# Transposing the retention operands one token block ahead, and splitting layer 1's output weights behind the GLA state chain

## The chip, the cores and the metric

The kernel runs on one core of a Trainium2 chip. The metric is the device time of one execution in microseconds (us), as the median of three runs. A core has a matrix engine (TensorE, PE in the profile), a vector engine (VectorE, DVE), a scalar engine (ScalarE, ACT), a general engine (GpSimd, POOL) and a sync engine (SyncE, SP) that issues most of the DMAs. PE writes to PSUM, the other engines take results from there.

## The reference

The kernel computes two layers of a diffusion backbone with model width 1024, for 512 latent tokens and 256 context tokens. Each layer projects the normalised tokens into three groups of heads (GLA, a gated linear attention; SSD, a state-space scan; retention), runs each as a scan in both directions, joins the outputs, projects them back and then runs a SwiGLU FFN. The two groups that matter here are instances of one scan, cut to its core:

```python
def chunked_scan(q, k, v, logg, s0):     # S_t = diag(exp(g_t)) S_{t-1} + k_t^T v_t,  o_t = q_t S_t
    def step(S, inp):
        qc, kc, vc, gc = inp
        G = jnp.cumsum(gc, axis=1)
...
        intra = jnp.einsum('bijh,bjhe->bihe', scores, vc)
        inter = jnp.einsum('bihd,bhde->bihe', qc * jnp.exp(G), S)
        G_last = G[:, -1:]
        S_new = jnp.exp(G_last[:, 0])[..., None] * S + jnp.einsum(
            'bjhd,bjhe->bhde', kc * jnp.exp(G_last - G), vc)
        return S_new, intra + inter
```

An output block is therefore a product inside the block (scores times values) plus a product of its queries with the state that enters it, once per direction. In the last layer only the four latent blocks are wanted as output; the two context blocks only feed the states.

## The kernel before

Tokens are handled in six blocks of 128: blocks 0 to 3 are latent, 4 and 5 context. Matrices of weights are loaded as fp32 into a buffer `raw`, of which there is one, and split into a high and a low part: ACT writes `whi`, DVE writes `wlo` as the rest. A product is then three matmuls (`gemm3`, L498): high by high, high by low, low by high.

The stage that is changed stands between the input projections and the FFN of each layer, and its code runs like this. `ret_gen` is a generator of the retention work, called by `pump()` from inside `gla_levels`, which builds the GLA scores level by level (L1016 to L1035: DVE, POOL and ACT make `XX`, PE multiplies it at L1028, DVE copies the masked result into `A` at L1035). For each output block `ret_out` does, on PE: four transposes of `qk` (L939); then, after DVE (L942) and ACT (L943, L944) have copied them to `rqT` in SBUF, the scores (L950), the products with the two states (L962), and, after DVE has multiplied the scores by their decay (`rA`, L953), the products with the values (L966); ACT copies the result to `vvg` (L968). `rqT` has one buffer.

After the retention come the GLA states. `gla_kv` (matmuls L1053, masked by DVE at L1057) makes what a block adds, `gla_step` (DVE, L1065) carries the state on, first backwards through the blocks, then forwards, and `gla_out` (L1073, L1077 on PE, L1083 on DVE) gives the outputs.

The output projection takes its weights in four units of 1024 by 256, loaded by `load_wo`: unit j is read into `raw` (L382) and split eight slices long (`whi` L394, `wlo` L395). `out_front` gates the joined block, transposes it (L1233), splits it into `H` (ACT L1235, DVE L1236) and multiplies it with the four units; the blocks are called positions 0 to 3 in layer 1. `out_back` normalises the rows (L283 and on), `load_gw` prepares a gain (POOL, L348).

The order on each engine isn't the order of the code: a scheduler simulates the program and takes, engine by engine, what it holds to be ready and due; the order within PE is filled up with matmuls of the remaining input projections (L498) where they fit. Engines work through their rows in that order. `tc.issue_after(x)`, used by the change, makes the instructions of the step's engine that are written inside it come behind instruction x in that order.

## Time and profile before

| what | us |
| --- | --- |
| median of three runs | 1889.72 |
| the three runs | 1876.48, 1889.72, 1896.44 |
| the profiled execution's own time | 1883.05 |
| its span, first to last instruction | 1881.3 |
| PE busy | 1744.7 |
| DVE busy | 1169.3 |
| ACT busy | 793.0 |
| POOL busy | 560.7 |

Times that are read from the profile belong to the profiled execution, which took 1883.05 us. The trace puts every instruction on its engine with a start and a length in microseconds from the start of the span, names what ended each wait, and gives the clock that TensorE was granted in any stretch as a share of its full speed (1.00 is 2.4 GHz, 0.50 is 1.2 GHz).

### The profile page before, as it was taken

How to read it: one execution, taken by the hardware profiler on the slowest of the kernel's cores; microseconds unless marked ns; L12 is line 12 of the kernel's file. 1: busy time of each engine (PE TensorE's matmuls, PEld its weight loads, DVE VectorE, ACT ScalarE, POOL GpSimd, SP SyncE). 2: the span in 40 equal slices, each digit the busy share in tenths (PEclk: the TensorE clock that was granted, in tenths of full speed). 3: DMA queues.
4: the chain of work that ended last, by engine and by line, in shares of the span. 5: the costliest groups of instructions: out<-in, count | busy, mean ns of one | idle time of the engine just before them, and what ended most of it. 6: DMA issues, size and time to landing. Idle time of an engine off the chain costs nothing. (4 is left out here: it accounts for less than half of the span.)

```text
span 1881.3 us, 30313 instructions
## 1 busy us (share of the span) xinstructions
PE 1744.7 (93%) x11851; PEld 1576.0 (84%) x11851; DVE 1169.3 (62%) x1981; ACT 793.0 (42%) x1433; POOL 560.7 (30%) x569
## 2 busy tenths in 40 slices
PE   4999999999879999999899989999987969999998
PEld 3778887798879999999788777889876969999886
DVE  4586787557557655554334446678766568888455
ACT  3545343225654333333323465444423544444343
POOL 1002622104303432332312240073312226555322
PEclk9999999999989999999999989999977989999999
DMA  8535457415325433332645374345613245444663
GB/s 277 183 103 171 136 188 262 156 46 177 113 68 145 140 105 93 93 93 90 240 140 184 116 235 134 112 147 171 214 53 124 84 129 153 125 138 130 245 209 128
DMA packets 239228, 275.15 MB, mean 146 GB/s; under 512 B 14056, under 2 KB 182476, under 8 KB 239084
## 3 DMA queue, kind: packets, MB, share of 16 engines
q1 hardware_dynamic: 237872, 271.30, 45.0%
q8 instruction: 93, 1.52, 0.3%
q10 hardware_dynamic: 1212, 1.91, 0.3%
q14 instruction: 51, 0.42, 0.1%
HBM read 234.24 MB, written 38.93 MB: 145 GB/s over the span
## 5 line engine op out<-in xcount | busy, mean ns | idle before, releaser
L369 DVE TENSOR_TENSOR wlo<-raw,whi 128x1024 fp32r<-128x1024 f32 (+2 forms) x192 | 264.1, 1382 | 160.0 <-ACT whi L368 159.7
L1324 PE MATMUL px<-H,whi 128*128 128x384 f32 (+1 forms) x1408 | 307.6, 310 | 7.4 <-ACT whi L368 7.3
L368 ACT CAST whi<-raw 128x1024 fp32r<-128x1024 f32 (+2 forms) x192 | 194.0, 1018 | 221.6 <-PE px L1324 86.3
L498 PE MATMUL mm<-whi,H 128*128 128x256 f32 x1376 | 275.5, 295 | 11.3 <-ACT stg L630 5.3
L498 PEld LDWEIGHTS mm<-whi,H 128*128 128x128 f32 x1376 | 224.1, 197 | 26.1 <-issue 12.7
L1324 PEld LDWEIGHTS px<-H,whi 128*128 128x128 f32 x1408 | 235.1, 190 | 10.2 <-ACT whi L368 9.5
L1324 PE MATMUL px<-H,wlo 128*128 128x384 f32 (+1 forms) x704 | 211.5, 310 | 0.9 <-DVE wlo L369 0.8
L498 PE MATMUL mm<-wlo,H 128*128 128x256 f32 x688 | 200.6, 292 | 0.0
L498 PE MATMUL mm<-H,whi 128*128 128x256 f32 (+2 forms) x640 | 160.9, 342 | 6.8 <-ACT xp L759 4.4
L368 ACT CAST whi<-S 128x1024 fp32r<-128x1024 f32 x88 | 73.5, 835 | 165.3 <-DVE S L419 84.6
L498 PEld LDWEIGHTS mm<-wlo,H 128*128 128x128 f32 x688 | 135.4, 197 | 3.1 <-issue 2.1
L1324 PEld LDWEIGHTS px<-H,wlo 128*128 128x128 f32 x704 | 131.6, 190 | 1.7 <-DVE wlo L369 1.7
L498 PEld LDWEIGHTS mm<-H,whi 128*128 128x128 f32 (+1 forms) x640 | 109.5, 190 | 26.0 <-ACT xp L759 6.2
L1278 POOL TENSOR_TENSOR hidlo<-hr,hidhi 128x768 fp32r<-128x768 f32 (+1 forms) x40 | 69.7, 1745 | 191.1 <-ACT hidhi L1277 184.7
L498 PE MATMUL px<-whi,H 128*128 128x256 f32 x640 | 120.5, 288 | 3.9 <-ACT H L1235 2.2
L1359 POOL TENSOR_TENSOR hf<-hf,g 128x384 f32<-128x384 f32 (+1 forms) x44 | 55.2, 1255 | 223.2 <-issue 147.0
L369 DVE TENSOR_TENSOR wlo<-S,whi 128x1024 fp32r<-128x1024 f32 x88 | 89.3, 1015 | 40.6 <-ACT whi L368 40.5
L1407 PE MATMUL px<-wlo,hidhi 128*128 128x512 f32 x276 | 108.7, 394 | 0.0
L498 PE MATMUL mm<-H,wlo 128*128 128x256 f32 (+3 forms) x320 | 108.3, 339 | 0.0
L1407 PE MATMUL px<-whi,hidhi 128*128 128x512 f32 x276 | 107.8, 393 | 0.0
L498 PEld LDWEIGHTS px<-whi,H 128*128 128x128 f32 x640 | 101.3, 193 | 6.3 <-ACT H L1235 3.2
L1407 PE MATMUL px<-whi,hidlo 128*128 128x512 f32 x276 | 106.1, 389 | 0.0
(334 smaller groups left out, 4086.0 us busy)
## 6 DMA issues: line engine op xcount, KB each, us to landing
raw<-ffn_w_dram SPq DMA_DIRECT2D x100, 512.0 KB
araw<-ada_w_dram SPq DMA_DIRECT2D x96, 512.0 KB
raw<-w_in_dram SPq DMA_DIRECT2D x26, 1024.0 KB
raw<-ffn_w_dram SPq DMA_DIRECT2D x20, 1024.0 KB
hr<-hd SPq DMA_DIRECT2D x22, 768.0 KB
hr<-hd SPq DMA_DIRECT2D x22, 512.0 KB
Rt<-gd SPq DMA_DIRECT2D x40, 256.0 KB
hd<-hf SPq DMA_DIRECT2D x22, 384.0 KB
```

The costliest lines, as they stand in the source:

```text
L368: S.copy(hi, src)
L369: lo_engine.tensor_tensor(lo, src, hi.bitcast(F32), ALU.subtract)
L498: PE.matmul(ps, x(k), y(k), start=(k == 0 and p == 0), stop=(k == total - 1 and p == 2))
L1278: (G if q else V).tensor_tensor(lo[:, q], hr[:, q], hi[:, q].bitcast(F32), ALU.subtract)
L1324: PE.matmul(ps[:, :hn], w[x][:, k], r[y](k), start=first and k == 0 and p == 0, stop=k == 3 and p == 2, skip_group_check=True)
L1359: G.tensor_tensor(h1, h1, g1, ALU.mult)
L1407: PE.matmul(ps, lh[x](k), rh[y](k), start=f + k == 0 and p == 0, stop=f + k == NF - 1 and p == 2, skip_group_check=True)
```

## The change

`ret_out` is cut in two. The new `ret_front` holds the transposes and the copies into `rqT`; it is called for the first output block ahead of the loop, and for every following block from inside the block before it, between the products with the states and the products with the values. In layer 1 `rqT` gets a second buffer. In layer 1, too, the splits of the output weights' units 1, 2 and 3 are held on DVE behind the fifth step of the GLA state chain (the last backward one; `steps` collects them, `chain` counts them). ACT's part of these splits is not held. No instruction is added or taken away.

```diff
-    def load(i, hp=None):
+    def load(i, hp=None, after=None):
...
-            for k in range(step):
-                w = cols[prem][:, 66 + k0 + k:67 + k0 + k]
-                S.activation(hi[:, k], raw[:, k0 + k], AF.Copy, scale=w)
-                V.scalar_tensor_tensor(lo[:, k], raw[:, k0 + k], w, hi.bitcast(F32)[:, k], ALU.mult, ALU.subtract)
+            with tc.issue_after(after) if after is not None else nullcontext():
+                for k in range(step):
+                    w = cols[prem][:, 66 + k0 + k:67 + k0 + k]
+                    S.activation(hi[:, k], raw[:, k0 + k], AF.Copy, scale=w)
+                    V.scalar_tensor_tensor(lo[:, k], raw[:, k0 + k], w, hi.bitcast(F32)[:, k], ALU.mult,
+                                           ALU.subtract)
...
-        def ret_out(tb, sf, sb):
-            qT = pt(Rp, "rqT", [128, 4, 2, 128], bufs=1)
+        def ret_front(tb):
+            qT = pt(Rp, "rqT", [128, 4, 2, 128], bufs=2 if last else 1)
...
             S.copy(qT[:, 0], pv[:, 0])
             S.copy(qT[:, 3], pv[:, 1])
+            return qT
+
+        def ret_out(tb, sf, sb):
+            qT = rq.pop(tb)
...
                     first = False
+            if tb != tbs_out[-1]:
+                nx = tbs_out[tbs_out.index(tb) + 1]
+                rq[nx] = ret_front(nx)
             for h in range(4):
                 PE.matmul(ps[:, 64 * h:64 * h + 64], A[:, h], vvg[:, tb, 256 + 64 * h:320 + 64 * h],
...
-                V.scalar_tensor_tensor(st, cur, g["dec"][d][:, i:i + 1], st, ALU.mult, ALU.add)
+                ins = V.scalar_tensor_tensor(st, cur, g["dec"][d][:, i:i + 1], st, ALU.mult, ALU.add)
+                steps.append(ins.ins)
...
             rf = None
+            rq[tbs_out[0]] = ret_front(tbs_out[0])
...
-            load(u["wo"][j], hp=None if j < 2 else wop)
+            load(u["wo"][j], None if j < 2 else wop, steps[chain - 1] if last and j else None)
...
                     gst_(t, t - 1 if t else None)
+                chain = len(steps)
```

The new text shifts line numbers: the retention's transposes, scores, state products and value products, L939, L950, L962 and L966 before, are L941, L956, L968 and L975 after; the level products L1028 become L1037, the projections' matmuls L498 become L500, the split L394 and L395 become L395 and L396, the GLA lines L1057, L1065 become L1066, L1074, and in the output projection L1208 to L1236 become L1220 to L1248.

On PE, in layer 1, this is the passage from the second to the third output block of the retention before the change (`rkv` are the states):

```order
L962 MATMUL px<-rkv_12817,rqT 128x128 x2
L962 MATMUL px<-rkv_12750,rqT 128x128 x2
L1028 MATMUL px<-XX 128x128 x4
L966 MATMUL px<-vvg,rA 128x64
L1028 MATMUL px<-XX 128x128 x2
L966 MATMUL px<-vvg,rA 128x64 x3
L1028 MATMUL px<-XX 128x128 x2
L939 MATMUL px<-cst,qk 128x128 x4
L950 MATMUL px<-rqT 128x128 x4
```

And the same passage, from the second output block to the third, after it:

```order
L968 MATMUL px<-rkv_12836,rqT 128x128 x2
L968 MATMUL px<-rkv_12773,rqT 128x128 x2
L500 MATMUL mm<-wlo,H 128x256
L941 MATMUL px<-cst,qk 128x128 x4
L1037 MATMUL px<-XX 128x128 x2
L500 MATMUL mm<-whi,H 128x256 x2
L975 MATMUL px<-vvg,rA 128x64
L1037 MATMUL px<-XX 128x128
L975 MATMUL px<-vvg,rA 128x64 x3
L1037 MATMUL px<-XX 128x128 x3
L500 MATMUL mm<-wlo,H 128x256
L500 MATMUL mm<-whi,H 128x256 x2
```

The transposes no longer stand directly ahead of the scores that need them, and matmuls of the last input projection (L500), which stood ahead of the first block before, stand between the blocks: 23 of them in the first of the three passages, 12 in the second, 5 in the third. In layer 0 the last three passages hold 44, 46 and 38 of these matmuls before and 14, 13 and 14 after, beside four transposes, four scores, four state products, four value products and eight level products in either; there, 141 of them now stand between the last GLA output and the first transposes of the output projection that follow.

On DVE, in layer 1, the GLA state chain before the change, from the third block's contribution on:

```order
L1057 TENSOR_TENSOR gkv_13202<-px,cst_10270 128x256
L395 SCALAR_TENSOR_TENSOR wlo<-raw,cols_645,whi 128x256
L1057 TENSOR_TENSOR gkv_13208<-px,cst_10270 128x512
L395 SCALAR_TENSOR_TENSOR wlo<-raw,cols_645,whi 128x256
L1065 SCALAR_TENSOR_TENSOR gkv_13202<-gkv_13196,gdec_12498,gkv_13202 128x256
L395 SCALAR_TENSOR_TENSOR wlo<-raw,cols_645,whi 128x256 x2
L1057 TENSOR_TENSOR gkv_13214<-px,cst_10270 128x512
L395 SCALAR_TENSOR_TENSOR wlo<-raw,cols_645,whi 128x256
L1057 TENSOR_TENSOR gkv_13219<-px,cst_10270 128x256
L395 SCALAR_TENSOR_TENSOR wlo<-raw,cols_645,whi 128x256
L1065 SCALAR_TENSOR_TENSOR gkv_13208<-gkv_13202,gdec_12498,gkv_13208 128x256
```

And after it, from the same block on to the first split:

```order
L1066 TENSOR_TENSOR gkv_13208<-px,cst_10270 128x512
L1074 SCALAR_TENSOR_TENSOR gkv_13202<-gkv_13196,gdec_12498,gkv_13202 128x256
L1066 TENSOR_TENSOR gkv_13214<-px,cst_10270 128x512
L1066 TENSOR_TENSOR gkv_13219<-px,cst_10270 128x256
L1074 SCALAR_TENSOR_TENSOR gkv_13208<-gkv_13202,gdec_12498,gkv_13208 128x256
L1074 SCALAR_TENSOR_TENSOR gkv_13219<-gkv_13191,gdec_12482,gkv_13219 128x256
L1074 SCALAR_TENSOR_TENSOR gkv_13214<-gkv_13208,gdec_12498,gkv_13214 128x256
L396 SCALAR_TENSOR_TENSOR wlo<-raw,cols_645,whi 128x256 x5
L1074 SCALAR_TENSOR_TENSOR gkv_13214<-gkv_13219,gdec_12482,gkv_13214 128x256
L396 SCALAR_TENSOR_TENSOR wlo<-raw,cols_645,whi 128x256 x3
```

The chain is no longer mixed with splits; the splits behind it are unit 1's, where those inside it before were unit 3's (and unit 2's ran just ahead of it).

On ACT, in layer 1, the rows between the last retention copy and position 0's `H`, after the change:

```order
L1220 ACTIVATE gt<-gt 128x512 x2
L1221 ACTIVATE zt<-zt 128x512
L1224 ACTIVATE zt,sy<-ys 128x512
L1225 ACTIVATE ys<-ys,rs 128x512
L1227 ACTIVATE zt<-vvg 128x512
L395 ACTIVATE whi<-raw,cols_645 128x256 x8
L1221 ACTIVATE zt<-zt 128x512
L1247 CAST H<-mm 128x512 x2
L1224 ACTIVATE zt,sy<-ys 128x512
L1227 ACTIVATE zt<-vvg 128x512
L1225 ACTIVATE ys<-ys,rs 128x512
L395 ACTIVATE whi<-raw,cols_645 128x256 x8
```

Unit 2's eight slices now stand ahead of position 0's `H` and unit 3's eight behind it; before, both units' slices stood ahead of it and ahead of L1215 (L1227 here). On SP the load of unit 2 into `raw` has moved behind the loads of `ys`, `gt` and `zt` of positions 0 and 1, and the load of unit 3 behind the loads of the rows `x`.

## Rows read from the trace of the kernel before

**Rows 1.** The page: busy time of the engines, and PE's clock in 40 slices.
```profile
PE 1744.7 (93%) x11851; PEld 1576.0 (84%) x11851; DVE 1169.3 (62%) x1981; ACT 793.0 (42%) x1433; POOL 560.7 (30%) x569
...
PEclk9999999999989999999999989999977989999999
```

**Rows 2.** Layer 1: window, length, busy PE, PEld, DVE, ACT, POOL, clock, DMA.
```profile
1370.00:1380.00 10.00, 10.00 (x85) 9.42 (x82) 6.90 (x22) 4.55 (x13) 0.00 (x0) 1.00 0.09 30
1380.00:1390.00 10.00, 7.99 (x55) 6.76 (x54) 6.99 (x20) 2.92 (x7) 1.74 (x4) 0.52 0.37 118
...
1430.00:1440.00 10.00, 3.69 (x13) 3.37 (x14) 7.24 (x17) 2.95 (x8) 0.00 (x0) 0.58 0.19 54
```

**Rows 3.** Waits from 1366 to 1460 us: engine, line, releaser, total, times, longest.
```profile
PE px L1073 <- DVE gkv L1065: 8.0, 1, 8.0
...
PE px L950 <- ACT rqT L944: 5.6, 3, 2.0
```

**Rows 4.** PE's timeline in layer 1: start, length, line, operands, idle before.
```profile
1382.86 1.11 PE L939 MATMUL px<-cst,qk 128*128 128x128 f32 x4
1385.99 1.22 PE L950 MATMUL px<-rqT 64*128 64x128 f32 x8 [2.01 <-ACT rqT L944]
...
1394.68 1.11 PE L939 MATMUL px<-cst,qk 128*128 128x128 f32 x4
...
1400.63 0.84 PE L1028 MATMUL px<-XX 32*128 32x128 f32 x8
...
1403.86 0.69 PE L939 MATMUL px<-cst,qk 128*128 128x128 f32 x4
```

**Rows 5.** PE's timeline after the retention, to the output projection's first two positions.
```profile
1414.02 2.07 PE L1028 MATMUL px<-XX 32*128 32x128 f32 x20
...
1436.31 2.05 PE L1073 MATMUL px<-gkv,qe 128*128 128x256 f32 x4 [7.99 <-DVE gkv L1065]
...
1449.72 0.39 PE L498 MATMUL px<-whi,H 128*128 128x256 f32 x1 [1.20 <-ACT H L1235]
...
1462.96 0.38 PE L498 MATMUL px<-whi,H 128*128 128x256 f32 x1 [0.38 <-ACT H L1235]
```

**Rows 6.** DVE's timeline in the GLA state chain of layer 1.
```profile
1427.31 0.42 DVE L1057 TENSOR_TENSOR gkv<-px,cst 128x256 f32<-128x256 f32 x1
1430.19 0.48 DVE L395 SCALAR_TENSOR_TENSOR wlo<-raw,cols,whi 128x256 fp32r<-128x256 f32 x1 [2.46 <-ACT whi L394]
1430.59 0.68 DVE L1057 TENSOR_TENSOR gkv<-px,cst 128x512 f32<-128x512 f32 x1
...
1435.68 1.78 DVE L1065 SCALAR_TENSOR_TENSOR gkv<-gkv,gdec,gkv 128x256 f32<-128x256 f32 x4
```

**Rows 7.** Unit 3's load on SP's queue, and its split on ACT.
```profile
1424.03 0.38 SPq L382 DMA_DIRECT2D raw<-w_out_dram  x1
...
1429.65 3.30 ACT L394 ACTIVATE whi<-raw,cols 128x256 fp32r<-128x256 f32 x8 [2.38 <-DMA raw<-w_out_dram]
```

**Rows 8.** Layer 0's output weights: load, ACT's split, DVE's split, POOL's gain beside it.
```profile
445.76 0.38 SPq L382 DMA_DIRECT2D raw<-w_out_dram  x1
...
453.06 3.31 ACT L394 ACTIVATE whi<-raw,cols 128x256 fp32r<-128x256 f32 x8 [4.56 <-DMA raw<-w_out_dram]
...
454.60 7.06 DVE L395 SCALAR_TENSOR_TENSOR wlo<-raw,cols,whi 128x256 fp32r<-128x256 f32 x7
...
456.37 5.01 POOL L348 TENSOR_TENSOR gw<-gw,xn 128x1024 f32<-128x1024 f32 x2 [4.90 <-DMA gw<-gts]
```

**Rows 9.** Windows of L498 alone: window, length, PE busy, PEld busy, clock.
```profile
1350.00:1355.00 5.00, 1.35 (x9) 1.15 (x10) 1.00 0.59 169
1355.00:1360.00 5.00, 1.58 (x12) 1.17 (x10) 1.00 0.56 199
1375.00:1380.00 5.00, 1.00 (x7) 0.65 (x5) 1.00 0.04 11
```

**Rows 10.** One window of layer 0's retention and GLA, all engines.
```profile
350.00:440.00 90.00, 90.00 (x737) 81.64 (x736) 50.51 (x128) 26.95 (x60) 15.00 (x26) 1.00 0.19 63
```

More of the change, by code (lines that the diff above doesn't have):

```diff
@@ L1 @@
-from contextlib import ExitStack
+from contextlib import ExitStack, nullcontext
 import numpy as np
@@ L1083, in gla_out @@
             V.tensor_tensor(vvg[:, tb, 0:256], y, ps[:, :256], ALU.add)
-        gA = {}
-        rkv, rb = {}, {5: None}
+        gA, steps = {}, []
+        rkv, rb, rq = {}, {5: None}, {}
         def ret_gen():
```

## The prediction

> **What bounds the kernel now.** The page comes first. PE is busy for 1744.7 of 1881.3 us, 93%, and no other engine above 62%, so nearly everywhere PE's own work sets the time and a change off PE is worth nothing [rows 1]. In the row of PE's clock the reader is to see the one deep dip, the slices that read 7 and 7 late in the line: one slice is 47 us, so they lie between 1364 and 1458 us. That is layer 1's retention and GLA, the stage of this change. Next come the windows there: until 1380 PE is fully busy at a clock of 1.00, then it is busy for 8 of 10 us at 0.52, and in 1430 to 1440 for 3.69 of 10 [rows 2]. So two losses overlap, waits and half speed. The waits name their releasers: three of them, 5.6 us together, are scores that wait for ACT's last copy into `rqT`, and one of 8.0 us is the first GLA output waiting for the state chain on DVE [rows 3]. Layer 0 does the same work in 350 to 440 us with PE busy for 90.00 of 90 us at 1.00 [rows 10]: there the change removes no wait of PE.
>
> **The change part by part.** I make the sum against the profiled execution, 1883.05 us (span 1881.3, the rest lies around it), and move its difference to the median, 1889.72, which is 6.7 us above it; the three runs themselves span 20 us, so nothing under 1% (19 us) can be told from no change.
>
> *The transposes, layer 1.* Each passage between blocks now reads transposes (L939), PE idle, scores (L950) [rows 4]. With the transposes ahead of the value products, these and the level products stand as cover over DVE's and ACT's copies: in the first passage of before, 7.5 us of products lie between the end of the scores (1387.21) and the next transposes (1394.68), and of these only the state products stay ahead of the transposes; the copies' wait is 2.01. The three waits go: -5.6 us [rows 3]. Their work is moved, not removed. What comes late next is `rA`, DVE's product between scores and value products; the state products, and now the transposes too, cover it. The second `rqT` buffer lets the copies start without waiting for the state products. If the cover were gone, the 5.6 would come back.
>
> *The clock, layer 1.* Without waits, the three passages from 1382.86 to 1414.02 hold 31.16 - 5.6 = 25.6 us of work, of which 1400.63 to 1404.55 ran at full speed [rows 4, 5]; so 21.6 us ran at half, and could shrink by 10.8. Whether they do hangs on what PE does there, and the matmuls of the projection, L498, now stand among them (23, 12 and 5). One costs 1.35/9 = 0.15 us at full clock [rows 9]. The rows show two stretches of mixed work to compare with: in 1350 to 1360, with 21 records of L498 among level products, the clock was 1.00 and stayed there; in 1375 to 1380 there were 7, and behind it the clock fell [rows 2, 9]. A passage has half of 9.8 us (11.82 less its 2.01 of waiting) = 4.9 us of other work at full clock. The first, 23 matmuls in 8.4 us, is nearest to the stretch that kept its clock, the third, 5 in 5.7 us, to the one behind which it fell, and the second, 12 in 6.7 us, lies between. Both ends: nothing regained, and 40 matmuls at half speed besides (+6.0), or 10.8 regained. I take the first passage alone at full speed, -4.9, and the 17 matmuls of the others at half speed, 17 x 0.15 = +2.6.
>
> *The state chain, layer 1.* DVE's rows show 7.95 us from the end of one L1057 (1427.73) to the last steps (1435.68); in them DVE idles 2.46 for `whi`, whose slices wait for unit 3's load, and eight splits stand between the chain's own instructions at 0.40 each (1430.19 to 1430.59) [rows 6, 7]. All of this leaves the chain: -(2.46 + 3.2) = -5.7. PE waits 7.99 for just this [rows 5], so the whole of it is on the path. Unit 2's eight splits stood ahead of the chain, beside the last level copies; they are worth between 0 and 3.2, as these copies were partly waiting for PE anyway, and I take the middle, -1.6.
>
> *What is given back.* DVE's splits of units 1 to 3 now start at the fifth step, before 1436.6 (1435.68 plus half of the last four steps' 1.78) [rows 6]. There is one `raw`, so each unit's load, on SP's queue, waits for the splits of the unit before it. From the fifth step: 3.2 for unit 1's splits and 0.4 for a step between them, 5.6 for unit 2's load (1424.03 to 1429.65), 3.3 for ACT's slices, which are queued ahead of position 0's `H` [rows 7], and 1.2 from `H` to the first matmul [rows 5]: 13.7 us, where it was 1449.72 - 1436.6 = 13.1. Thus the GLA outputs, which set this stretch before, are overtaken by the weights: +0.6. Unit 3 follows: its load can start at some 12.9, its first slice is split at 12.9 + 5.6 + 0.8 = 19.3, and position 0, which takes about 12 us (the 13.24 between the first matmuls of two positions, less the 1.2), needs it after three quarters, at 13.7 + 9 = 22.7 [rows 5]. So 3.4 us remain, and the loads of the FFN's weights behind it on SP have longer still. Layer 0's load took 7.3 (445.76 to 453.06) [rows 8], so one load may be late by 1.7 and shift all of it. And seven splits took 7.06 us there, not 2.8, while POOL wrote two gains in 5.01: 4.3 longer, 2.1 for the one gain of layer 1. Ends: 0 and 3.8; I take 1.7, the slower load. Together +2.3.
>
> The Trainium skill, "SBUF — State Buffer", section "SBUF: two separate sides", has it that VectorE and GpSimd share a pair of ports which whoever comes first holds for a whole instruction. Layer 0's seven splits agree with it [rows 8]; by that rule the late splits meet POOL's gain surely, and the sum would lose the 2.1 as well, 10.8 in the place of 12.9.
>
> *Layer 0.* Its waits aren't in the retention, but the order moves: the fill goes from the passages (44 to 14 in each of the last three) to the stretch ahead of the output projection, 141 x 0.15 = 21 us. At full clock this is neutral. The output weights' splits then lie beside other work; what can be won or lost is bounded by those seven splits' 4.3 us, either way. I take 0.
>
> **The sum:** -5.6 - 4.9 + 2.6 - 5.7 - 1.6 + 2.3 = -12.9 us: 1870.2 for the profiled execution, 1876.8 on the median.
>
> **The rivals.** *The clock stays up through all of layer 1's passages:* -5.6 - 10.8 - 7.3 + 2.3 = -21.4, 1868.3. For it speaks that PE will have no waits there; against it, that the fall at 1380 came behind 10 us in which PE was busy without a gap [rows 2], and that the third passage is made of nearly the same matmuls as before. The Trainium skill, "TensorE: Matmul & The Clock Gate", section "HAM oscillation — how this bites in real kernels", lays such falls to stretches in which TensorE idles, so that taking the waits away would give this rival. This trace shows a fall without one.
>
> *The clock doesn't come back and the weights come late:* -5.6 + 6.0 - 7.3 + 2.3 = -4.6 with the weights as I took them, and -2.5 with the other end of what is given back (0.6 + 3.8); some -3, 1886.7. For it speaks that the scores, level and value products are the same matmuls that ran at 0.5 before.
>
> *Slower, through layer 0:* the last three passages there, 14 matmuls of L498 (2.1 us) beside 4.9 us of other work, fall to half speed as layer 1's did. Each then takes 14 us and not 7: +21.0, and with the -12.9 of layer 1 +8.1, 1897.8. It decides at the point where such a passage loses its full clock. Against it, 14 in 7.0 us is near the 21 in 10 us of the stretch that stayed at 1.00; for it, that stretch had other products beside the level products, and what never fell in layer 0 before had about 44 in 11.5 us [rows 9, 10].
>
> That the change doesn't do what it says is excluded: the order shows the moved rows on PE, DVE, ACT and SP.
>
> **How the numbers follow.** Forecast 0.45, full clock 0.20, clock and weights 0.20, layer 0 slower 0.15. The predicted time is the forecast's, 1876.8. The range reaches down to 1864, a little under the full-clock case with layer 0's 4.3 on its side, and up to 1895, over the weights' case and most of the way to the slower one. Faster by over 1% means under 1870.8: two thirds of the full-clock case (0.13) and a fifth of the forecast (0.09), 0.22. Slower by over 1%, above 1908.6, takes layer 0 falling for longer than three passages: 0.07. Within 1%: 0.71.
>
> **What would show it.** After: no wait of L956 for `rqT`; no split between L1066 and L1074, and the wait of the GLA outputs (8.0) down to 2 or so; clock 1.00 for the first passage, about 0.5 in the third; the first output matmul 13 to 14 us behind the fifth step, waiting for ACT's `H`, and this in turn for the load; clock 1.00 in layer 0's retention. Wrong would be: a wait of that size on `rA` or on PSUM, a clock under 0.9 between 350 and 440 us, or a period of positions 0 to 1 well above 15 us.

## The result and the profile after

The changed kernel takes 1905.18 us (median of four runs, 1893.48 to 1915.39) and the one before 1890.01 (four runs, 1876.48 to 1896.44): a ratio of 1.0105, interval 1.0068 to 1.0142. It is slower by one per cent, where 1876.8 had been forecast, and it lies above the range. The profiled execution took 1896.16 us with a span of 1894.4, 13.1 more than before. The four executions had spans of 1894.4, 1912.4, 1891.7 and 1913.6 us at mean granted clocks of 0.955, 0.946, 0.956 and 0.947: of the 20 us between the two pairs some 18 are half speed, and the profiled execution is one of the shorter pair.

The page of the kernel after, busy time of the engines and PE's clock in 40 slices:

```profile
PE 1765.8 (93%) x11851; PEld 1592.7 (84%) x11851; DVE 1165.9 (62%) x1981; ACT 792.7 (42%) x1433; POOL 562.9 (30%) x569
...
PEclk9999999999898999999999989999978979999999
```

The number of instructions is the same as in [rows 1], and PE is busy for 21.1 us longer with them. The row of the clock doesn't tell where: the slices over layer 0's retention (350 to 440 us) read 9 in both kernels, since one slice is 47 us and averages a fall of 10 us away. The new 8 in the 11th slice lies at 474 to 521 us, behind the retention, and the 8 of the 12th has moved to the 13th. The dip in layer 1 is still there.

One window over layer 0's stage, from 330 us, where the two kernels still stand at the same place, to its last transposes of L306, before and then after (columns as in [rows 2]):

```profile
330.00:552.20 222.20, 203.75 (x1656) 186.40 (x1652) 124.79 (x285) 92.23 (x197) 49.19 (x66) 0.97 0.35 118
```

```profile
330.00:568.80 238.80, 220.94 (x1644) 200.61 (x1636) 123.64 (x285) 92.07 (x197) 50.01 (x66) 0.92 0.33 108
```

The stage grew by 16.6 us. PE's idle time in it didn't (18.4 before, 17.9 after, length less busy time): no wait was won or lost. What changed is the clock. The time lost by it is taken as the length times what the clock lacks of 1.00, PE's waits counted in; summed over windows of 5 us it is 7.4 us before and 19.0 after. So 11.6 of the 16.6 us are half speed. Narrower windows of the kernel after show where:

```profile
350.00:360.00 10.00, 10.00 (x77) 8.58 (x76) 5.49 (x18) 1.93 (x5) 0.76 (x2) 1.00 0.05 16
...
370.00:380.00 10.00, 10.00 (x54) 8.98 (x54) 7.94 (x17) 2.56 (x5) 2.21 (x5) 0.52 0.08 22
...
420.00:430.00 10.00, 10.00 (x53) 9.10 (x53) 3.33 (x8) 1.94 (x3) 1.45 (x2) 0.75 0.15 39
...
460.00:470.00 10.00, 7.08 (x33) 6.59 (x34) 6.88 (x16) 7.51 (x17) 3.68 (x4) 0.66 0.56 170
...
500.00:510.00 10.00, 8.16 (x50) 8.16 (x51) 7.60 (x16) 9.10 (x18) 6.19 (x6) 0.66 0.64 209
```

Of these the reader is to see the second: PE is busy for 10.00 of 10 us and runs at 0.52. Nothing in PE's busy column tells it from the window in the first row; the count of matmul records does (54, not 77). And the same 90 us as in [rows 10]:

```profile
350.00:440.00 90.00, 90.00 (x602) 79.17 (x600) 51.66 (x127) 20.76 (x45) 14.39 (x26) 0.91 0.12 38
```

PE is busy for 90.00 us as before, with 602 matmul records in place of 737.

In layer 1 the same stage, from the L306 transposes ahead of it to those at its end, before and after:

```profile
1110.00:1514.50 404.50, 371.06 (x2744) 329.50 (x2743) 269.65 (x547) 181.45 (x372) 104.49 (x140) 0.92 0.42 133
```

```profile
1126.70:1525.70 399.00, 373.11 (x2743) 331.27 (x2742) 267.55 (x546) 180.99 (x371) 104.70 (x140) 0.93 0.42 134
```

It gained 5.5 us: PE's idle time fell by 7.5 (33.4 to 25.9) and its busy time rose by 2.1. With layer 0's +16.6 this is +11.1 of the +13.1; the rest, 1.9, stands behind layer 1's stage (1894.4 - 1525.7 against 1881.3 - 1514.5). What became of layer 1's waits, from 1390 to 1490 us of the kernel after:

```profile
PE px L500 <- ACT H L1247: 3.9, 1, 3.9
PE mm L1245 <- DVE gt L1234: 2.4, 1, 2.4
...
PE px L1083 <- DVE gkv L1074: 1.7, 1, 1.7
```

The three waits for `rqT` (5.6 in [rows 3]) are gone, and the wait for the state chain has gone from 8.0 to 1.7. In their place stand a wait for `gt` ahead of position 0's transposes and one for position 1's `H`. PE's timeline shows the two new ones and the first output matmul:

```profile
1440.33 1.10 PE L1083 MATMUL px<-gkv,qe 128*128 128x256 f32 x4 [1.69 <-DVE gkv L1074]
...
1452.79 0.69 PE L1245 MATMUL mm<-cst,gt 128*128 128x128 f32 x2 [2.37 <-DVE gt L1234]
...
1454.58 0.58 PE L500 MATMUL px<-whi,H 128*128 128x256 f32 x1
...
1471.98 0.39 PE L500 MATMUL px<-whi,H 128*128 128x256 f32 x1 [3.89 <-ACT H L1247]
```

From the first output matmul of position 0 to that of position 1 it is 17.4 us, where [rows 5] have 13.24. ACT's and DVE's rows say what stands ahead of the `gt` and the `H`; ACT first:

```profile
1449.49 3.30 ACT L395 ACTIVATE whi<-raw,cols 128x256 fp32r<-128x256 f32 x8 [3.54 <-DMA raw<-w_out_dram]
...
1462.77 3.31 ACT L395 ACTIVATE whi<-raw,cols 128x256 fp32r<-128x256 f32 x8 [2.63 <-DMA raw<-w_out_dram]
...
1468.59 0.63 ACT L1224 ACTIVATE zt<-ys 128x512 f32<-128x512 f32 x1 [0.90 <-DVE ys L1222]
...
1471.36 1.06 ACT L1247 CAST H<-mm 128x512 fp32r<-128x512 f32 x2
```

And DVE's:

```profile
1450.87 1.27 DVE L396 SCALAR_TENSOR_TENSOR wlo<-raw,cols,whi 128x256 fp32r<-128x256 f32 x3
1452.05 0.68 DVE L1234 TENSOR_TENSOR gt<-gt,hss 128x512 f32<-128x512 f32 x1
...
1463.31 3.28 DVE L396 SCALAR_TENSOR_TENSOR wlo<-raw,cols,whi 128x256 fp32r<-128x256 f32 x8 [1.59 <-ACT whi L395]
1467.15 1.41 DVE L1222 TENSOR_TENSOR ys<-ys,zt 128x512 f32<-128x512 f32 x1 [0.56 <-ACT zt L1221]
```

Three splits of unit 2 stand directly ahead of position 0's `gt`. The eight of unit 3 stand ahead of position 2's `ys` (position 1's `gt` was done at 1461.7, ahead of them). Position 1's `H` is late on ACT: it stands there behind unit 3's slices, which wait for their load, and behind position 2's gating, which waits for that `ys`.

### The profile page after: what moved, and what is told of

It reads as the page before. It is cut to its first block, busy times and chain, and to the rows that moved or that the text cites. A ratio compares the mean times of both kernels' runs of the same rounds, so it can differ in the third digit from the quotient of the medians.

```text
span 1894.4 us, 30305 instructions
## 1 busy us (share of the span) xinstructions
PE 1765.8 (93%) x11851; PEld 1592.7 (84%) x11851; DVE 1165.9 (62%) x1981; ACT 792.7 (42%) x1433; POOL 562.9 (30%) x569
## 4 chain that ended last, share of the span: by engine, by line
PE 64%; DMA 14%; DVE 10%; ACT 5%; issue 3%; POOL 3%; SPq 0%; POOLq 0%; ACTq 0%; DVEq 0%
PE px L1336 17%; PE mm L500 16%; PE px L1419 6%; PE mm L1336 6%; PE px L500 5%; DMA raw<-ffn_w_dram 5%; DVE wlo L369 3%; PE px L1037 2%; DMA qd<-stg 2%; DMA araw<-ada_w_dram 2%; PE mm L1419 2%; ACT whi L368 2%; DMA raw<-w_out_dram 1%; DMA raw<-w_in_dram 1%; PE pa L203 1%
## 5 line engine op out<-in xcount | busy, mean ns | idle before, releaser
L500 PE MATMUL mm<-whi,H 128*128 128x256 f32 x1376 | 283.7, 299 | 12.7 <-ACT stg L632 6.7
L500 PEld LDWEIGHTS mm<-whi,H 128*128 128x128 f32 x1376 | 227.8, 199 | 31.2 <-issue 13.7
L500 PE MATMUL mm<-wlo,H 128*128 128x256 f32 x688 | 203.5, 296 | 0.0
L500 PE MATMUL mm<-H,whi 128*128 128x256 f32 (+2 forms) x640 | 161.2, 342 | 6.6 <-ACT xp L761 5.5
L500 PEld LDWEIGHTS mm<-wlo,H 128*128 128x128 f32 x688 | 137.2, 199 | 3.3 <-issue 2.5
L500 PE MATMUL px<-whi,H 128*128 128x256 f32 x640 | 125.1, 295 | 8.3 <-ACT H L1247 4.5
L500 PEld LDWEIGHTS mm<-H,whi 128*128 128x128 f32 (+1 forms) x640 | 109.4, 190 | 26.4 <-ACT xp L761 7.4
L500 PEld LDWEIGHTS px<-whi,H 128*128 128x128 f32 x640 | 104.9, 200 | 11.4 <-ACT H L1247 5.7
L500 PE MATMUL mm<-H,wlo 128*128 128x256 f32 (+3 forms) x320 | 108.5, 339 | 0.0
```

The costliest lines, as they stand in the source:

```text
L500: PE.matmul(ps, x(k), y(k), start=(k == 0 and p == 0), stop=(k == total - 1 and p == 2))
```

## The experiments

The diffs are against the changed kernel unless the text names another, and show the lines that matter. Ratios are to the kernel before, from runs on the same chip, with the 95% interval. The theory after the result was: layer 0's retention runs at half speed because the order moved the projections' matmuls out of it; layer 1's gains are real and partly given back. The rivals were that layer 0's part costs nothing and layer 1's weights come so late that they cost the per cent, and that the falls of the clock wander from execution to execution and the change has no part in them.

**Fronts ahead in layer 0 alone.** Layer 1 keeps the order of before, in both parts.

```diff
...
-            qT = rq.pop(tb)
+            qT = ret_front(tb) if last else rq.pop(tb)
...
-            if tb != tbs_out[-1]:
+            if not last and tb != tbs_out[-1]:
...
-            load(u["wo"][j], None if j < 2 else wop, steps[chain - 1] if last and j else None)
+            load(u["wo"][j], None if j < 2 else wop, None)
```

> Only layer 0's transposes go ahead; layer 1 is as before, both in order and in weights. Theory A (the loss is layer 0's new order: matmuls of the projection leave the retention, the scores and level products are cut into more and shorter groups, and the clock falls in this stage): slower than before by 14 to 22 us, 1.0075 to 1.0115, with the clock at half speed somewhere between 360 and 430 us and the first out-projection transposes some 17 us later than 443.6. Rival B (the falls of the clock wander from execution to execution and the change has no part in it): within 5 us of before.

It gave 1.0127 (1.0100 to 1.0154): all of the loss, from a part that was to cost nothing. Its window over layer 0's stage:

```profile
330.00:581.50 251.50, 232.94 (x1666) 210.28 (x1664) 123.61 (x285) 92.44 (x198) 50.05 (x66) 0.89 0.32 104
```

and the 90 us of [rows 10] in it:

```profile
350.00:440.00 90.00, 90.00 (x547) 77.69 (x547) 41.67 (x107) 17.18 (x36) 9.56 (x20) 0.79 0.11 36
```

Half speed costs 28.0 us here (again over windows of 5 us), 20.6 more than before. This is the longest of six executions; what half speed takes in all of them stands in the table at the end of this section.

**Layer 1 alone, both parts.** Layer 0 keeps the order of before.

```diff
-            qT = rq.pop(tb)
+            qT = rq.pop(tb) if last else ret_front(tb)
...
-            if tb != tbs_out[-1]:
+            if last and tb != tbs_out[-1]:
```

> Both parts of the change, in layer 1 alone; layer 0 as before. Theory A: layer 1's gain in the profile stands by itself, 5 us (the waits of 5.6 and 6.3 us less 5.3 us of new waits in the output projection and some slower matmuls), so 0.995 to 1.000, and layer 0's clock at 1.00 from 350 to 440 us. Rival B: as far off as the changed kernel, 1.005 to 1.015.

1.0009 (0.9986 to 1.0031): no gain that can be measured, and just above the 0.995 to 1.000 expected. With the 1.0127 of layer 0 the two halves make 1.0136, within the interval of the whole change. PE's waits in its layer 1:

```profile
PE mm L1246 <- DVE gt L1235: 3.8, 1, 3.8
PE px L500 <- ACT H L1248: 3.6, 3, 3.0
...
PE px L500 <- DVE H L1249: 2.1, 3, 0.7
```

These are the new waits for `gt` and `H` again, 9.5 us together.

**The transposes ahead in layer 1 alone,** the weights split as before.

```diff
-            qT = rq.pop(tb)
+            qT = rq.pop(tb) if last else ret_front(tb)
...
-            if tb != tbs_out[-1]:
+            if last and tb != tbs_out[-1]:
...
-            load(u["wo"][j], None if j < 2 else wop, steps[chain - 1] if last and j else None)
+            load(u["wo"][j], None if j < 2 else wop, None)
```

> Only layer 1's transposes go ahead; the weights are split as before. If the transposes' cover is what I took it for, the three waits for rqT (5.6 us) go and the state chain's 8.0 us stay; the scores are cut apart by projection matmuls, which gives 1 to 2 us back: 0.996 to 0.999. If the cut scores and the clock eat it all: 0.999 to 1.002.

0.9965 (0.9947 to 0.9982), -6.6 us. This part gains by itself.

**The weights alone.** No front ahead in either layer.

```diff
-            qT = rq.pop(tb)
+            qT = ret_front(tb)
...
-            if tb != tbs_out[-1]:
+            if False and tb != tbs_out[-1]:
...
-            rq[tbs_out[0]] = ret_front(tbs_out[0])
```

> Only layer 1's weight splits go behind the state chain; the transposes stay. The chain's wait falls from 8.0 to about 1.7 us. If the output projection's new waits (5.3 us in the changed kernel: 2.9 in front of its matmuls, 2.4 in front of its transposes) come from the late weights, they are here too, and the time is within 2 us of before: 0.999 to 1.001. If they come from the transposes' part, the gain of 6 us stands: 0.995 to 0.998.

0.9976 (0.9957 to 0.9994), -4.5 us. The gain stands, and yet the wait for `gt` is here too (2.4 us), so that it comes with the weights and not with the transposes. Each part of layer 1 gains, and both together don't. The summary of the output projection's matmuls (first and last start) shows where the gain goes; the kernel before, with the transposes alone, with the weights alone, and with both:

```profile
L498 PE MATMUL px<-whi,H x256: 278/283/388, 1449.7 to 1501.0; 128*128 128x256 f32 x128
```

```profile
L500 PE MATMUL px<-whi,H x256: 278/283/387, 1435.2 to 1486.5; 128*128 128x256 f32 x128
```

```profile
L500 PE MATMUL px<-whi,H x256: 274/283/582, 1450.4 to 1504.7; 128*128 128x256 f32 x128
```

```profile
L500 PE MATMUL px<-whi,H x256: 277/283/581, 1434.2 to 1496.7; 128*128 128x256 f32 x128
```

The projection takes 51.3, 51.3, 54.3 and 62.5 us. Its start is counted from the last of the L306 transposes ahead of the stage (1109.7, 1103.0, 1113.6 and 1108.8), since the spans differ up to there: 340.0 us before, 7.8 earlier with the transposes alone, 3.2 with the weights alone, 14.6 with both. So the gains ahead of the output projection do add up, and more; but with both, 11.2 of the 14.6 are given back in it. One window over the projection, before and with both, says by what:

```profile
1449.70:1501.00 51.30, 50.90 (x423) 50.28 (x424) 27.94 (x49) 27.72 (x55) 14.72 (x15) 1.00 0.36 123
```

```profile
1434.20:1496.70 62.50, 56.38 (x425) 54.32 (x424) 30.51 (x60) 31.94 (x65) 14.71 (x15) 0.92 0.33 111
```

PE's idle time grew by 5.7 us (0.4 to 6.1), the waits for `H` above, and 5.0 are half speed; for the weights themselves PE waits nowhere. In the changed kernel the start is 11.7 earlier (1454.6 less 1126.3), the projection takes 57.6, and 6.3 are given back: 4.0 of idle time and 2.3 of half speed. The profiled execution with both parts is one of the shorter of its twelve (a span of 1876.9, 4.4 under before's), so that it still shows some gain where the median shows none.

**Only unit 3 held back.** Units 1 and 2 are split as before; the transposes ahead in layer 1 alone.

```diff
-            load(u["wo"][j], None if j < 2 else wop, steps[chain - 1] if last and j else None)
+            load(u["wo"][j], None if j < 2 else wop, steps[chain - 1] if last and j == 3 else None)
```

> Layer 1's transposes ahead, as in the changed kernel; layer 0 as before; and of the weight splits only unit 3's are held behind the state chain, so that units 1 and 2 are split early and their loads no longer wait for the chain. If layer 1's gain was lost in the chain of load, split and load again (unit 2's load after unit 1's splits, unit 3's after unit 2's), the chain's wait stays at about 2 us, the 8.8 us of waits in front of the output projection's transposes and matmuls fall to 2 or 3 us, and the time is 9 to 13 us under before: 0.993 to 0.996. Rival: the two parts don't add because the clock falls elsewhere in their place; then it is no better than the transposes alone, 0.996 to 0.999.

And the same on the kernel before, with nothing else:

```diff
-            load(u["wo"][j], hp=None if j < 2 else wop)
+            load(u["wo"][j], None if j < 2 else wop, steps[chain - 1] if last and j == 3 else None)
```

> Only unit 3's splits are held behind the state chain; transposes as before, in both layers. By the same theory the chain's 8.0 us fall to about 2 and nothing is given back: 4 to 7 us under before, 0.9965 to 0.998. If holding units 1 and 2 as well costs nothing, the same as the kernel that holds all three (0.9976).

They gave 0.9960 (0.9939 to 0.9980), at the edge between its theory and its rival, and 0.9987 (0.9966 to 1.0007), which misses the 0.9965 to 0.998 expected. The second is no better than all three units held (0.9976), so that by itself it decides nothing. With the transposes ahead, one unit held beats three (0.9960 against 1.0009, the intervals apart), and it is not to be told from none held (0.9965). So with the transposes ahead holding the weights is worth nothing, and holding all three costs.

**The projections' matmuls brought forward.** On the kernel with fronts ahead in layer 0 alone, the projections that fill layer 0's retention are given a higher priority, so that they run ahead of it and none is left to stand in the passages.

```diff
-        proj_b("gr", tbs_out, to_dram(rds[l], 0))
-        proj_b("rg", tbs_out, to_dram(rds[l], 256))
-        for j in range(2):
-            proj_b(f"z{j}", tbs_out, to_dram(zds[l], 256 * j))
+        with tc.high_priority(offset=1000) if not last else nullcontext():
+            proj_b("gr", tbs_out, to_dram(rds[l], 0))
+            proj_b("rg", tbs_out, to_dram(rds[l], 256))
+            for j in range(2):
+                proj_b(f"z{j}", tbs_out, to_dram(zds[l], 256 * j))
```

> Layer 0's transposes ahead, layer 1 as before; and the projection matmuls of layer 0 that follow the retention in the code are raised in priority, so that they all run ahead of the retention: its last three passages hold none of them, and the scores are no longer cut apart. Theory clock (what the stage lost is full speed, since the fill is gone from the passages): no better than the kernel with 14 of them in each passage, 1.010 to 1.020, with 0.5 in most of the last three passages. Theory cut (what it lost is the cutting of scores and level products into short groups): 8 us better than that kernel, 1.005 to 1.009, and the scores back at half their time.

1.0213 (1.0185 to 1.0241), the worst of all and a little above either theory's range. In the last three passages, with scores at 450, 458, 466 and 473 us here, no matmul of the projections is left; in the first two, from 422, some still stand. Windows ahead of the passages, in the first two, and from the last three on:

```profile
360.00:370.00 10.00, 10.00 (x48) 5.87 (x49) 2.46 (x6) 0.63 (x1) 0.91 (x2) 0.54 0.40 120
...
420.00:430.00 10.00, 9.95 (x91) 8.45 (x89) 3.71 (x15) 2.42 (x7) 0.76 (x2) 1.00 0.05 15
430.00:440.00 10.00, 10.00 (x80) 8.70 (x80) 6.55 (x18) 2.00 (x5) 2.00 (x4) 1.00 0.04 13
...
456.00:466.00 10.00, 10.00 (x61) 8.58 (x62) 6.61 (x18) 2.57 (x7) 0.92 (x3) 0.66 0.18 63
466.00:476.00 10.00, 10.00 (x66) 8.71 (x66) 5.50 (x15) 1.65 (x4) 0.74 (x2) 0.70 0.00 0
476.00:486.00 10.00, 10.00 (x36) 8.27 (x33) 5.02 (x12) 6.22 (x13) 1.18 (x2) 0.50 0.43 132
```

The first two passages ran at 1.00. Of the three without these matmuls the first did too up to 456, and the other two ran at half speed for about half of their time, with PE busy throughout: the sign that the clock's theory had named, in part. The scores of all three stand in one group, so that a loss doesn't need their cutting. But much of the half speed lies ahead of the retention, where matmuls of the projections run among level products (0.54 in 360 to 370). "A passage with few of these matmuls falls to half speed" is thereby too simple a rule; that moving them about moves the half speed stands.

**Work added to layer 0.** On the kernel with fronts ahead in layer 0 alone, four matmuls of 128 by 512 behind each of its next fronts, 20 in all, whose results nothing reads. Work is added and none taken out.

```diff
                 rq[nx] = ret_front(nx)
+                if not last:
+                    pd = px()
+                    for _ in range(4):
+                        PE.matmul(pd, qk[:, tb, 0:128], qk[:, tb], start=True, stop=True)
```

> Layer 0's transposes ahead, layer 1 as before, and in each of layer 0's five passages four added matmuls (queries of the block by its whole row, 128 by 512, fp32) whose results nobody reads: work added, not taken out. They cost some 0.85 us each at full speed, 17 us in all. Theory clock: PE keeps full speed from 350 to 430 us, and the added work is partly paid back by it, 1.010 to 1.018 in total, with half speed gone from this stretch. Theory cut alone: the 17 us come on top, 1.018 to 1.024, and the clock falls as without them.

To have their price, the same 20 matmuls on the kernel before:

```diff
+            if not last and tb != 3:
+                pd = px()
+                for _ in range(4):
+                    PE.matmul(pd, qk[:, tb, 0:128], qk[:, tb], start=True, stop=True)
```

> The kernel before, with the same twenty matmuls (128 by 512, fp32, read by nobody) added in the same five passages of layer 0's retention: work added, not taken out. There the clock was at 1.00 all along, so nothing can be paid back and this measures their price. Theory clock: they cost their full time, 14 to 17 us, 1.0075 to 1.009, so that adding them behind the transposes ahead (1.0080 against 1.0127) paid back some 20 us. Rival: they cost little anywhere, since they fill hidden idle time of PE; then 1.000 to 1.003, and their gain there says nothing of the clock.

On the kernel before they cost 0.58% (1.0058, 1.0040 to 1.0077), 10.9 us, between the two ranges expected. On the one with fronts ahead they don't cost, they gain: 1.0080 (1.0051 to 1.0110) where it was 1.0127 without them (on another chip), some 9 us, and it lies below the range of either theory. The rows of that kernel, the stage, the 90 us and the added matmuls (two records each):

```profile
330.00:563.60 233.60, 217.66 (x1680) 193.75 (x1676) 123.74 (x285) 92.15 (x197) 51.70 (x66) 0.96 0.34 110
```

```profile
350.00:440.00 90.00, 90.00 (x640) 73.44 (x639) 47.30 (x121) 17.10 (x36) 14.91 (x26) 1.00 0.12 38
```

```profile
L977 PE MATMUL px<-qk 128*128 128x512 f32 x40 | 18.0, 592 | 0.0
```

The clock is 1.00 where it was 0.79, and the time lost to half speed in the stage falls from 28.0 to 9.0 us. In these profiled executions PE does 20 matmuls more and ends the stage 17.9 us earlier.

**Scores uncut.** On the kernel with fronts ahead in layer 0 alone, the scores of a block are made one piece that the order can't cut; this leaves more of the projections' matmuls in the last three passages of layer 0 (21 in each). First in both layers, then in layer 0 alone.

```diff
-            for pr in range(2):
-                for h in range(2):
-                    rr = slice(64 * h, 64 * h + 64)
-                    PE.matmul(ps[h][:, 128 * pr:128 * pr + 128], qT[rr, 3, pr], qT[rr, 0, pr],
-                              start=True, stop=True)
+            with nullcontext() if last else tc.tile_critical():
+                for pr in range(2):
+                    for h in range(2):
+                        rr = slice(64 * h, 64 * h + 64)
+                        PE.matmul(ps[h][:, 128 * pr:128 * pr + 128], qT[rr, 3, pr], qT[rr, 0, pr],
+                                  start=True, stop=True)
```

> Layer 0's transposes ahead, layer 1's transposes as before, and in both layers the four scores of a block are kept together as one group; the scheduler then also leaves 21 projection matmuls and not 14 in each of layer 0's last three passages. The kernel without this stands at 1.0127. If the cutting of the scores matters by itself, they fall back from 7 or 8 us to 4 in layer 0: 1.009 to 1.011. If the fill matters as well, the half-speed time between 350 and 440 us falls from 37 us to under 20, and the time is 1.000 to 1.008. If neither: 1.011 to 1.015.

> As the kernel before this one, but the scores are kept together in layer 0 alone, since keeping them together in layer 1 made that stage 13 us longer in the profile. Layer 0's transposes ahead, 21 projection matmuls in each of the last three passages, scores in one group. If layer 0's loss was the cut scores and the half speed that came with the thinner fill, both are mostly gone, and the time is 1.000 to 1.005, with layer 0's stage up to 6 us longer than before's 222 us. If another cost of the transposes ahead remains in layer 0: 1.007 to 1.012.

In both layers it gave 1.0093 (1.0066 to 1.0120): layer 0's stage came down to 227.8 us, but layer 1's, which was to stay, grew by 13, so the run doesn't answer the question. In layer 0 alone it gave 1.0037 (1.0021 to 1.0054). Its stage and its 90 us:

```profile
330.00:555.60 225.60, 203.95 (x1651) 186.55 (x1650) 120.78 (x285) 92.08 (x197) 49.91 (x66) 0.96 0.35 115
```

```profile
350.00:440.00 90.00, 86.85 (x699) 77.52 (x696) 54.48 (x137) 26.50 (x58) 18.05 (x29) 1.00 0.19 62
```

So of layer 0's 1.27%, 0.90% (17 us; the two ran on different chips) goes when the clock comes back, here without added work, and although PE now idles for 3.15 us in the 90. Half speed costs 8.6 us in this stage, not 28.0. The edit changed both the uncut scores and the number of matmuls between them, and doesn't tell these two apart.

**Work added to layer 1.** Transposes ahead in layer 1 alone, unit 3 alone held back, and three unread matmuls behind each next front there, nine in all.

```diff
                 rq[nx] = ret_front(nx)
+                pd = px()
+                for _ in range(3):
+                    PE.matmul(pd, qk[:, tb, 0:128], qk[:, tb], start=True, stop=True)
```

> Layer 1's transposes ahead and unit 3's splits held (0.996), and three of the added matmuls behind the transposes in each of layer 1's three passages, 7.7 us of work added. If full speed can be kept there as in layer 0, the 24 us at half speed behind 1390 shrink and pay back up to 10.8 us: 0.993 to 0.996. If the later stretch falls all the same, they cost up to their price: 0.997 to 1.000.

0.9928 (0.9905 to 0.9951), -13.6 us: the fastest kernel of the study, where the same without the nine matmuls had 0.9960. Its windows over the second and third passage (scores from 1387.5 to 1406.3) and behind them:

```profile
1390.00:1400.00 10.00, 10.00 (x68) 7.62 (x67) 6.37 (x17) 3.36 (x8) 0.76 (x2) 1.00 0.01 2
1400.00:1410.00 10.00, 9.72 (x71) 7.34 (x69) 5.47 (x16) 3.51 (x9) 0.94 (x2) 1.00 0.04 13
1410.00:1420.00 10.00, 7.74 (x58) 6.62 (x58) 8.80 (x25) 5.89 (x12) 2.03 (x4) 0.64 0.70 238
```

and in the changed kernel, where the second and third passage lie from 1399.2 to 1422.3:

```profile
1400.00:1410.00 10.00, 10.00 (x40) 8.43 (x39) 2.65 (x6) 1.12 (x3) 0.00 (x0) 0.50 0.00 1
1410.00:1420.00 10.00, 10.00 (x52) 8.73 (x51) 4.23 (x11) 3.16 (x8) 0.84 (x2) 0.59 0.01 2
```

The profiled execution of the kernel without the nine has half speed there as well, from 1391 to 1414. The intervals of 0.9928 and 0.9960 overlap a little, and they come from different chips. That the nine matmuls pay for themselves is borne out by the clock over all executions (table below); that they gain the full 0.3% is likely, not more.

**More of it.** Three more behind the last block and three behind the last contributions to the GLA states.

```diff
+                if last:
+                    pd = px()
+                    for _ in range(3):
+                        PE.matmul(pd, vvg[:, 3, 256:384], vvg[:, 3], start=True, stop=True)
```

> As the kernel with three added matmuls in each of layer 1's passages, and three more behind the last retention block's state products and three behind the last GLA contributions, where PE waits 2 us for the state chain: 13 us of work added in all. Theory clock: layer 1 keeps full speed from the retention to the GLA outputs, some 45 us at half speed shrink to 10, 17 us are paid back: 0.990 to 0.995. Rival: no more is paid back than they cost, 0.996 to 1.000.

0.9950 (0.9924 to 0.9975), at the edge between the two: the time is no better. Over all executions half speed takes next to nothing less than with the nine alone (18.0 and 17.1 us under the kernel before), so the six matmuls' price isn't paid back, and PE waits 3.0 us for position 0's `gt`, 2.5 without them.

**The nine matmuls without the transposes ahead,** on the kernel before.

```diff
+            if last and tb != 3:
+                pd = px()
+                for _ in range(3):
+                    PE.matmul(pd, qk[:, tb, 0:128], qk[:, tb], start=True, stop=True)
```

> The kernel before, with three added matmuls (128 by 512, fp32, read by nobody) in each of layer 1's three passages, transposes and weights as before. If the gain of the kernel with transposes ahead, unit 3 held and these matmuls (0.9928, against 0.996 without them) is mostly the clock's, they gain by themselves: 0.994 to 0.998. If full speed can only be kept where PE doesn't wait for the transposes, they cost their price, 5 to 8 us: 1.002 to 1.005.

1.0046 (1.0026 to 1.0066): they cost. The waits for `rqT` are still there, 7.5 us of them now, and the clock goes to 0.73, 0.84, 0.74 and 0.60 from 1380 to 1420:

```profile
PE px L950 <- ACT rqT L944: 7.5, 3, 3.2
```

So the gain of 0.9928 needs the transposes ahead first, and the matmuls only then.

**Half speed over all executions.** Profiles show one execution each, but every execution has its span and its mean granted clock on record, and the span times what this clock lacks of 1.00 is the time at half speed, waits counted in, as above. Means over all executions less those of the kernel before on the same chip, in us, each uncertain by some 2 to 4:

| kernel | span | half speed | rest |
| --- | --- | --- | --- |
| fronts ahead in layer 0 alone | +22.5 | +15.6 | +6.9 |
| the same, 20 matmuls added | +15.4 | 0.0 | +15.3 |
| the kernel before, the same 20 added | +10.9 | -4.0 | +15.0 |
| fronts ahead in layer 0, its scores uncut | +7.8 | +0.1 | +7.7 |
| the same fronts, projections brought forward | +40.4 | +25.8 | +14.6 |
| layer 1 alone, unit 3 held | -6.2 | -8.7 | +2.5 |
| the same, nine matmuls added | -12.4 | -17.1 | +4.7 |

The executions of one kernel differ (81 to 103 us at half speed in the first one's six, 70 to 89 in 29 of the kernel before), so the falls do wander; but the means differ with the kernel, and that answers the rival. Two thirds of what layer 0's part costs are half speed, and both edits that bring the clock back bring all of this back. Some 7 us are something else.

## Why the prediction was wrong

**The step that failed is layer 0's:** "At full clock this is neutral", and with it "I take 0". The order had shown that the projections' matmuls leave the retention of layer 0, and they were counted as work that is moved and costs the same elsewhere. The bounds beside it, 4.3 us either way, were those of seven splits of weights and not of the moved matmuls. The runs showed in its place 11.6 us of half speed in the changed kernel's layer 0 and 28.0 - 7.4 = 20.6 with the fronts ahead there alone; two different edits that bring the clock back, one of which adds work, take 9 and 17 us off. Half speed is therefore shown as the cause of the greater part, 15.6 of 22.5 us over all executions of that kernel; why the clock falls in the new order is not.

The rival "slower, through layer 0" had stage and cause, and a chance of 0.15. Its place and its deciding point were wrong: it had the last three passages at half speed, and these (scores from 387 to 412 us) ran at 0.97 to 1.00 up to 410, while the falls came in 370 to 380 and from 418 on. It took passages without any of these matmuls to bring two of them to half speed there, and then for about half of their time. What the rows of before could have told is in [rows 2]: in 1380 to 1390, against the expectation that only waits cost the clock, the fall came behind ten us without one. I had read this for layer 1, and not asked it of layer 0, where PE had no wait to lose and 30 matmuls to lose in each passage.

Some 5 us of layer 0's 16.6 aren't half speed by the sum above, and some 7 of the 22.5 over all executions. The scores stand in two groups of four records there with other matmuls between, but in the run with the 20 added matmuls, where they do so too, this remainder is missing (233.6 - 9.0 less the 12.4 that the same matmuls add to the stage of the kernel before, at 227.2 against 214.8 without what half speed costs), and in the table too (15.3 against their price of 15.0), while with the scores uncut it stands (7.7). It stays open. So does which make-up of a stretch keeps the clock.

**The transposes, layer 1 (-5.6): right.** All three waits are gone, and `rA` came late nowhere by more than 0.3 us. By itself the part gave -6.6 us, which is this term and little more.

**The clock, layer 1 (-4.9 + 2.6): right in kind, and worth little.** The first passage, 1386 to 1398, ran at full speed and the second at half, as put; the third, put at half, was back at full speed from 1418 on. The stage's clock went from 0.92 to 0.93, and PE's busy time in it rose by 2.1 us where these terms had it fall by 2.3. The place of the falls isn't firm either: in the profiled execution of layer 1's two parts alone, the same text for layer 1, the second passage was back at full speed after 6 us (1383 to 1389) and the third ran at it throughout.

**The state chain (-5.7 - 1.6): right on its wait,** 8.0 to 1.7, and the weights alone gave -4.5 in all, which is these terms less 2.8.

**The give-back (+2.3): the right place, too small.** The first output matmul came 14.1 us behind the fifth step (1454.58 less the end of the step's group of three, 1440.5; forecast 13.7). But PE waited there for `gt` and not for `H`, 2.4 us that weren't foreseen, and the period of positions 0 to 1 grew by 4.2 and not by 1.7. Unit 3 was reckoned to be needed for the last quarter of position 0 only; on ACT its slices also stand ahead of position 1's `H`, with position 2's gating between, and its load took 8.0 us where the slower one reckoned with took 7.3. POOL's gain, which might have cost 2.1 more, met none of the held splits: it ran from 1456.5 to 1458.9, between unit 2's and unit 3's. In all 6.3 us were given back inside the output projection, and 11.2 with layer 1's two parts alone, which reaches it earlier; 2.3 and 5.0 of these are half speed, which the term didn't hold at all. That term was a fixed price; in these three profiles it grows with what the other terms win (3.0, 6.3 and 11.2 given back where the start was 3.2, 11.7 and 14.6 earlier). It is the second step that was mis-sized, and it is much of why the two parts, -6.6 and -4.5 us each by itself, are worth nothing together.

**The sum:** -12.9 was forecast and +13.1 measured in the profiled executions: +16.6 for layer 0, -5.5 for layer 1, +1.9 behind it. The medians differ by 15.2.

## What to carry to other kernels

Where PE has no wait, taking waits out of the order can only change what stands beside what: look at where the filler goes, and read the granted clock next to the busy share, since PE at 0.52 was busy for 10.00 of 10 us. When a change holds one thing back to hurry another, what is held back is late by more the more the rest wins, so its price has to be worked out against the changed stretch and not the old one. And where the clock falls in dense-looking work without waits, a few unread matmuls are a cheap trial, which in layer 1 paid only once the waits were gone. One profile is one execution: where the clock wanders, compare means of the granted clock over many before a single trace is believed.

## What the runs showed of the hardware

Added work made a kernel faster twice: 20 matmuls that cost 10.9 us on the kernel before took some 9 off another (1.0127 to 1.0080), and nine went with the best time of all (0.9928).

The clock fell without any idle time of PE: 0.52 in 370 to 380 us of the changed kernel, 0.50 in 1400 to 1410, 0.54 in 360 to 370 of the run with the projections brought forward, each with PE busy for all of it. Where it falls the runs don't let one foretell: without a matmul of the projections one passage of layer 0 ran at 1.00 up to 456 us and the next at 0.50 from 457 to 463, and layer 1's second fell to 0.50 with 12 of them in it. It is also not the same in every execution: the changed kernel's four differ by up to 20 us at half speed (83 to 103).

Two loads of a unit of output weights, of the same size, took 5.3 us and then 8.0 in one execution, from the issue to the first slice on ACT (1449.49 and 1462.77 above). SP's queue in the kernel after:

```profile
1444.21 0.38 SPq L382 DMA_DIRECT2D raw<-w_out_dram  x1
...
1454.79 0.38 SPq L382 DMA_DIRECT2D raw<-w_out_dram  x1
```
